# A pad of 320 bytes at one end of the on-chip memory, and one buffer fewer for a scratch tile of the query rotation

## The chip, the cores and the metric

The kernel runs on one core of one Trainium2 chip. The time is device microseconds of that core, the median of several executions. Beside it stands one profiled execution, from which all rows of the trace come.

## The reference

One step of a one-layer hybrid encoder in float32. A prompt of 1024 frames and 8 running streams of 16 frames (1152 rows, nine tiles of 128) go through the same layer:

```
h = rmsnorm(x) @ w_in                  # split in xr, gate, q, k, v, qi, ki, wi
y_a = rglru(conv(xr)) * gelu(gate)     # recurrent group, width 512
y_b = attention of rope(rmsnorm(q)), rope(rmsnorm(k)), v
      over the 256 (132) keys that qi, ki, wi select by their scores
x = x + concat(y_a, y_b) @ w_out
x = x + (silu(g) * u) @ w_ffn_out      # g, u = rmsnorm(x) @ w_ffn_in, inner width 2816
```

Keys, values, index keys and the recurrent states are outputs too.

## The kernel before

The program is one core's, recorded by a helper, so nearly all vector, scalar and pool instructions carry line 66 and nearly all matmuls line 207 (`mm`), 212 (`mm4`, plain float32) or 217 (transposes); they are told apart by the tiles they write and read.

**Matmuls.** A float32 factor is split in a high and a low part (`split`, `hi`, `lo`), both of a 4-byte type that the matmul takes as it is, and one product is three matmuls (`mm3`): high by high and both mixed ones. Each matmul loads its 128 stationary columns anew. In a row of the trace `ps<-hf,w 128*128 128x384` the moving tile comes first (`hf`, 384 columns), then the stationary one (`w`, 128 columns); in `ps<-w,a` the moving tile is `w2` (shown as `w`), the stationary one `a`.

**Stages, by the trace's time.** 0 to 73 us: norm, keys and values (`wk`). To 185: index scores (`ki`, `qeo`). To 372: the recurrent group (`h` moving, `w` stationary), with the first half of the queries beside it. To 408: the second half of the queries (`q_tile`, nine tiles of 24 matmuls with 256 moving columns, `w,h`). 408 to 475: the first half of the output product (`out_tile_a`, `wa,yF`), while the keys are rotated (`k_rope`) and the masks of the selection are made. To 653: attention. To 713: second half of the output product (`out_tile`, `w,rest`) with the second norm. To 1543: the feed-forward part (`ffn`), 22 slices of 128 inner columns. `ffn1` makes one slice: 2 weight columns, 3 thirds of the rows, 24 matmuls each, 144 in all. `ffn2` adds two slices into the result: 108 matmuls of 512 moving columns, eleven times.

**Rotation buffers.** `rope` takes a scratch tile, lets POOL write its two halves (`rp<-qn,tab`), and VectorE multiplies the query tile by the table (`qn<-qn,tab`) and adds the scratch tile (`qn<-qn,rp`):

```python
t2 = pool.tile([128, H, 64], F32, tag="rp", name="rp", bufs=bufs)
```

With two buffers POOL may write the scratch tile of the next query tile while VectorE still has to read that of this one. `k_rope` already calls it with one.

**Where tiles lie.** The memory of a partition is allotted from two ends. The lower end holds `h`, `hf`, `rest`, `smr`, `acc`, `ki`; the upper end, from the top down, the raw weights, the eight slots `w`, then what each stage needs. In `ffn` two weight tiles in ten and one `w2` tile in six go to free room in `rest` at the lower end (`slot1`, `slot2`):

```python
k = slots[0] % 10
if k % 5:
    return self.wslot(shape)
return rest[k // 5].rearrange("p (a x n) -> p a x n", a=4, x=2)
```

The built program's addresses, as remainder modulo 512 bytes (the row steps inside these tiles are whole multiples of 512 bytes, except `wk`, whose rows are 1312 bytes):

| tile | lies at | remainder |
|---|---|---|
| `h`, `hf`, `rest`, `smr`, `ki` | 1696 to 124,575 | 160 |
| `w` (8 slots), `raw` | 188,384 to 229,343 | 480 |
| `w2`, `a`, `sg` in `ffn` | 141,280 to 188,383 | 480 |
| `wk` | 109,792 to 130,783 | 224 at its start |
| `vhl` | 155,168 | 32 |
| `k1`, `k2` | 90,688 and 98,880 | 64 |

**Order.** Generators are interleaved by a planner in the kernel (`run`), and a scheduler of the framework then orders every engine's queue. Each engine takes its queue in order.

Of the kernel before, what the change touches and what calls it, by code (L numbers as in the profile page):

```python
# [9 lines left out]
F32 = mybir.dt.float32  # L10
# [71 lines left out]
class Kernel:  # L82
# [183 lines left out]
    def build(self, upto=99):  # L266
        ctx, tc, nc, I, O = self.ctx, self.tc, self.nc, self.I, self.O
        L = "left"
        R = "right"
# [2 lines left out]
        self.dram = ctx.enter_context(tc.tile_pool(name="dram", bufs=1, space=bass.MemoryType.DRAM))  # L272
        right, yst, mid, tka, kist = (ExitStack() for _ in range(5))
        pool = lambda st, name, side, bufs=1: st.enter_context(tc.tile_pool(name=name, bufs=bufs, side=side))
        self.raw = pool(right, "raw", R, 2)
        self.wr = pool(right, "wr", R, self.SLOTS)
        yF_p = pool(yst, "yF", R)
# [930 lines left out]
    def q_tile(self, i, half, tp, gq):  # L1208

        nc = self.nc  # L1210
        w, = yield from self.wait_w(("q", half))
        tab = self.tables(tp, i, gq, 2)
        pq = self.ps()
        for d in range(ND):
            ww = w[d // 2]
            self.mm3(pq[:, :256], self.h_lhs(i, d, 0), self.h_lhs(i, d, 1), ww[:, d % 2, 0, :],
                     ww[:, d % 2, 1, :], d == 0, d == ND - 1)
        if i == NT - 1:
            self.wused -= 4
        self.n_q += 1  # L1220
        self.begin()
        x = self.qn[:, i, half * 256:half * 256 + 256]
        nc.scalar.activation(x, pq[:, :256], AF.Copy)
        t = self.end()
        for h in range(4):
            sq = tp.tile([128, 64], BF16, tag="sq", name="sq")
            nc.scalar.activation(sq, pq[:, h * 64:h * 64 + 64], AF.Square, scale=0.125,
                                 accum_out=self.qss[:, i, 4 * half + h:4 * half + h + 1])
        yield 0.0
        yield from self.until(t)  # L1230
        x = x.rearrange("p (h d) -> p h d", h=4)
        self.rope(x, x, tab, 4, tp)

    def q_norm(self, tp):

# [515 lines left out]
```

## Time and profile before

| | |
|---|---|
| median of 3 runs | 1549.23 us (1546.99 to 1549.92) |
| the profiled execution's own time | 1549.64 us |
| its span, first to last instruction | 1547.9 us |
| TensorE busy | 1479.1 us (96%), 7786 matmuls |
| VectorE, ScalarE, POOL busy | 866.1, 619.5, 269.3 us |
| feed-forward stage | 712.8 to 1543.4 us |

The rows below come from views of that one execution. In the timeline of an engine each row merges consecutive instructions of one kind; the difference between the start of a row and the start of the next one, divided by the count, is the time from one matmul to the next. That is the rate; the duration of a single matmul (338 ns mean for `hf,w`) is longer, as matmuls overlap.

### The profile page before, as it was taken

The page shows a single profiled execution, that of the slowest core. Times are in us where ns is not written, and L with a number is a line of the kernel's source. Part 1 is how long each engine was busy: PE and PEld are TensorE (multiplying, and loading weights), DVE is VectorE, ACT ScalarE, POOL GpSimd, SP SyncE. Part 2 cuts the span into 40 slices and gives each one's busy share as a digit, 9 for nine tenths or more (in the row PEclk, how much of TensorE's full clock was granted, in tenths as well). Part 3 has the DMA queues.
Part 4 walks back from the last instruction along what each step waited for, and adds up shares of the span by engine and source line. Part 5 has one row for each costly group of instructions (what it writes and reads, how often), then busy time and mean ns, then how long its engine had stood idle before and what let it go on. Part 6 is the DMA issues. An engine that isn't in the chain of part 4 may idle for free.

```text
span 1547.9 us, 20878 instructions
## 1 busy us (share of the span) xinstructions
PE 1479.1 (96%) x7786; PEld 1314.3 (85%) x7786; DVE 866.1 (56%) x1904; ACT 619.5 (40%) x1481; POOL 269.3 (17%) x425
## 2 busy tenths in 40 slices
PE   6889899889997999999999999999999999999998
PEld 6877688778745788889999898989898989898987
DVE  7556899899968987677233334242424242515133
ACT  5447988978315878655202020202121111111100
POOL 4214233334764545200000000000000000000000
PEclk8999899999998999999999999999999999999999
DMA  7201111011410002123102020202011111101003
GB/s 240 58 16 31 46 37 30 4 31 57 153 41 11 1 28 58 39 56 92 46 0 82 1 82 4 79 20 63 27 55 31 51 42 41 55 28 55 28 0 122
DMA packets 95093, 75.24 MB, mean 49 GB/s; under 512 B 13380, under 2 KB 85828, under 8 KB 94992
## 3 DMA queue, kind: packets, MB, share of 16 engines
q1 hardware_dynamic: 94992, 73.91, 15.8%
q8 instruction: 61, 1.00, 0.3%
q14 instruction: 40, 0.33, 0.1%
HBM read 67.62 MB, written 6.27 MB: 48 GB/s over the span
## 4 chain that ended last, share of the span: by engine, by line
PE 75%; DVE 10%; ACT 6%; issue 4%; POOL 2%; DMA 2%; SPq 0%; ACTq 0%; DVEq 0%; POOLq 0%
PE ps L207 68%; PE ps L212 4%; DVE junk L66 4%; PE ps L217 3%; ACT jk L66 3%; DVE tk_cand L66 2%; ACT L66 1%; DVE tr L66 1%; ACT tr L66 1%; DMA gk<-in_k_norm_dram 0%; ACT relu L66 0%; DMA x<-in_x_prompt_dram 0%; POOL m L66 0%; DVE s L66 0%; DVE m L66 0%
## 5 line engine op out<-in xcount | busy, mean ns | idle before, releaser
L207 PE MATMUL ps<-hf,w 128*128 128x384 f32 x2556 | 460.5, 338 | 0.0
L207 PEld LDWEIGHTS ps<-hf,w 128*128 128x128 f32 x2556 | 451.5, 187 | 0.8
L207 PE MATMUL ps<-w,a 128*128 128x512 f32 x999 | 239.1, 390 | 0.0
L66 DVE TENSOR_TENSOR acc<-ps,acc 128x512 f32<-128x512 f32 x234 | 161.0, 690 | 120.3 <-PE ps L207 119.2
L207 PEld LDWEIGHTS ps<-w,a 128*128 128x128 f32 x999 | 187.4, 188 | 40.1
L66 ACT ACTIVATE w<-raw 128x512 fp32r<-128x512 f32 x124 | 75.2, 628 | 300.5 <-PE ps L207 220.9
L66 DVE TENSOR_TENSOR sg<-ps,sg 128x384 f32<-128x384 f32 x66 | 36.7, 557 | 279.9 <-PE ps L207 279.3
L66 DVE TENSOR_TENSOR w<-raw,w 128x512 fp32r<-128x512 f32 x116 | 76.8, 687 | 85.2 <-ACT w L66 85.0
L66 ACT ACTIVATE a<-sg 128x384 fp32r<-128x384 f32 x66 | 34.5, 523 | 220.8 <-DVE sg L66 220.8
L207 PE MATMUL ps<-hf,rest 128*128 128x384 f32 x612 | 114.5, 334 | 0.0
L66 ACT ACTIVATE jk<-s,tk_cand 128x384 bf16<-128x384 f32 (+3 forms) x128 | 99.5, 777 | 32.4 <-DVE tk_cand L66 29.6
L207 PE MATMUL ps<-h,w 128*128 128x384 f32 x576 | 107.1, 343 | 0.0
L207 PEld LDWEIGHTS ps<-hf,rest 128*128 128x128 f32 x612 | 106.9, 188 | 0.2
L207 PEld LDWEIGHTS ps<-h,w 128*128 128x128 f32 x576 | 100.8, 188 | 3.9 <-ACT relu L66 0.2
L207 PE MATMUL ps<-w,h 128*128 128x256 f32 (+1 forms) x600 | 97.0, 318 | 0.0
L207 PEld LDWEIGHTS ps<-w,h 128*128 128x128 f32 x600 | 84.3, 192 | 6.6 <-issue 0.2
L66 ACT ACTIVATE sg<-ps 128x384 f32<-128x384 f32 x66 | 32.1, 486 | 122.0 <-PE ps L207 122.0
L212 PE MATMUL ps<-wa,yF 128*128 128x512 f32 x144 | 64.9, 605 | 2.7 <-DVE tk_cnt L66 2.7
L66 POOL TENSOR_SCALAR m<-m,mx 128x128 f32<-128x128 f32 (+7 forms) x64 | 51.7, 816 | 53.6 <-DVE mx L66 42.7
L212 PEld LDWEIGHTS ps<-wa,yF 128*128 128x128 f32 x144 | 27.1, 194 | 36.0 <-issue 30.3
L207 PE MATMUL ps<-smr,vhl 128*128 128x512 f32 x162 | 54.0, 418 | 2.3 <-ACT smr L66 1.4
L66 ACT ACTIVATE m<-m,mx 128x128 f32<-128x128 f32 (+7 forms) x64 | 49.3, 770 | 16.1 <-DVE mx L66 15.7
(266 smaller groups left out, 2142.0 us busy)
## 6 DMA issues: line engine op xcount, KB each, us to landing
raw<-in_w_ffn_in_dram SPq DMA_DIRECT2D x44, 512.0 KB, 4.8
raw<-in_w_ffn_out_dram SPq DMA_DIRECT2D x22, 512.0 KB, 3.6
raw<-in_w_in_dram SPq DMA_DIRECT2D x16, 512.0 KB, 5.0
out_dram<-acc SPq DMA_DIRECT2D x9, 512.0 KB, 2.6
x<-in_x_prompt_dram SPq DMA_DIRECT2D x8, 512.0 KB
acc<-in_x_prompt_dram SPq DMA_DIRECT2D x8, 512.0 KB
tab<-in_rope_dram SPq DMA_DIRECT2D x43, 64.0 KB, 1.8
wa<-in_w_out_dram SPq DMA_DIRECT2D x4, 512.0 KB
```

What stands on the lines that cost most here:

```text
L66: return f(*args, **kw)
L207: self.nc.tensor.matmul(out, lhsT, rhs, start=start, stop=stop)
L212: self.nc.tensor.matmul(out, lhsT, rhs, start=start, stop=stop)
L217: self.nc.tensor.transpose(out, in_, self.ident[0:n, 0:n])
```

## The change

A pool with one tile of 80 floats per partition (320 bytes), which nothing uses, is opened at the upper end ahead of all others, so everything at the upper end lies 320 bytes lower. The rotation of the query tiles takes one scratch buffer (1024 bytes) where it took two, which leaves the stage of the recurrent group and the queries the room; the tiles of that stage then lie 704 bytes higher.

```diff
         pool = lambda st, name, side, bufs=1: st.enter_context(tc.tile_pool(name=name, bufs=bufs, side=side))
+        pool(right, "pad", R).tile([128, 80], F32, name="pad_r")
         self.raw = pool(right, "raw", R, 2)
...
         x = x.rearrange("p (h d) -> p h d", h=4)
-        self.rope(x, x, tab, 4, tp)
+        self.rope(x, x, tab, 4, tp, bufs=1)
```

Remainders after: `w`, `raw`, `w2`, `a`, `sg` 160 (were 480), `vhl` 224 (was 32), `k1` and `k2` 256 (were 64), `wk` 416 at its start (was 224); the lower end keeps 160. Counts of instructions stay as they were on TensorE, and up to about 375 us of the trace every queue keeps its order. From the query tiles to the first attention tile the scheduler orders some queues differently.

POOL, late in the query tiles: `rp` is the scratch tile, `tab` the table of sines and cosines, scaled by `gq`; `tt`, `tr` and `yF` are tiles of the recurrent group (minus: before, plus: after).

```order
-L66 TENSOR_TENSOR rp<-qn,tab 128x4x32 x4
+L66 TENSOR_TENSOR rp<-qn,tab 128x4x32 x2
 L66 TENSOR_SCALAR tt<-tt 128x384 x3
 L66 MEMSET tr 128x1
-L66 TENSOR_TENSOR tab<-tab,gq 128x128
+L66 TENSOR_TENSOR rp<-qn,tab 128x4x32 x2
 L66 MEMSET tt 128x8
-L66 TENSOR_TENSOR rp<-qn,tab 128x4x32 x2
-L66 TENSOR_TENSOR tab<-tab,gq 128x128
-L66 TENSOR_TENSOR rp<-qn,tab 128x4x32 x2
+L66 TENSOR_TENSOR tab<-tab,gq 128x128
 L66 TENSOR_TENSOR yF<-yF,tr 128x384
```

Before, POOL wrote the scratch tiles of two query tiles one after the other; now other work, or a wait for VectorE, stands between two of them, and every later query tile stands one to three places further back.

VectorE, where the masks of the first selection group end and the first results of the output product are added (`jk`, `tk_cnt`: the mask; `acc`: the result tile):

```order
-L66 SCALAR_TENSOR_TENSOR ps<-jk_912,ps 128x256
-L66 TENSOR_TENSOR acc<-ps,acc 128x512
+L66 SCALAR_TENSOR_TENSOR ps<-jk_916,ps 128x256
+L66 TENSOR_TENSOR qn<-qn,tab 128x256
 L66 TENSOR_TENSOR tk_cnt<-tk_cnt,ps 128x1
 L66 TENSOR_TENSOR acc<-ps,acc 128x512
-L66 TENSOR_TENSOR qn<-qn,tab 128x256
+L66 TENSOR_TENSOR qn<-qn,rp 128x256
 L66 TENSOR_SCALAR tk_cnt<-tk_cnt 128x1
-L66 TENSOR_TENSOR qn<-qn,rp 128x256
```

Before, the fifteenth of 18 query tiles had been rotated ahead of this point and the sixteenth stood behind it; now the fourteenth stands here.

TensorE, in the same stage, before and after:

```order
L212 MATMUL ps<-wa,yF 128x512 x12
L217 MATMUL ps<-ident,kn 128x128
L212 MATMUL ps<-wa,yF 128x512 x6
L217 MATMUL ps<-ident,kn 128x128
L212 MATMUL ps<-wa,yF 128x512 x6
```

```order
L212 MATMUL ps<-wa,yF 128x512 x8
L217 MATMUL ps<-ident,kn 128x128
L212 MATMUL ps<-wa,yF 128x512 x8
L217 MATMUL ps<-ident,kn 128x128
L212 MATMUL ps<-wa,yF 128x512 x8
```

The transposes of the rotated keys (`ident,kn`) stand at slightly other places among the matmuls of the output product; nothing else moves on TensorE.

## Rows read from the trace of the kernel before

**Rows 1.** The page: granted TensorE clock by slices, chain by line.

```profile
PEclk8999899999998999999999999999999999999999
...
PE ps L207 68%; PE ps L212 4%; DVE junk L66 4%; PE ps L217 3%; ACT jk L66 3%; DVE tk_cand L66 2%; ACT L66 1%; DVE tr L66 1%; ACT tr L66 1%; DMA gk<-in_k_norm_dram 0%; ACT relu L66 0%; DMA x<-in_x_prompt_dram 0%; POOL m L66 0%; DVE s L66 0%; DVE m L66 0%
```

**Rows 2.** Stretches: length, busy PE, PEld, DVE, ACT, POOL (counts), clock, DMA, GB/s.

```profile
712.80:1543.40 830.60, 830.60 (x4373) 781.36 (x4371) 295.33 (x471) 143.78 (x268) 0.00 (x0) 1.00 0.15 45
...
408.00:480.00 72.00, 66.08 (x163) 29.23 (x161) 49.90 (x109) 14.10 (x48) 40.68 (x72) 0.98 0.11 34
```

**Rows 3.** Timeline of PE, feed-forward: start us, us, what, count.

```profile
739.58 2.25 PE L207 MATMUL ps<-hf,rest 128*128 128x384 f32 x12
741.66 6.52 PE L207 MATMUL ps<-hf,w 128*128 128x384 f32 x36
748.02 2.25 PE L207 MATMUL ps<-hf,rest 128*128 128x384 f32 x12
...
790.22 24.64 PE L207 MATMUL ps<-w,a 128*128 128x512 f32 x108
814.70 4.40 PE L207 MATMUL ps<-hf,w 128*128 128x384 f32 x24
...
865.34 1.52 PE L207 MATMUL ps<-w,a 128*128 128x512 f32 x6
866.70 0.86 PE L207 MATMUL ps<-rest,a 128*128 128x512 f32 x3
867.40 2.22 PE L207 MATMUL ps<-w,a 128*128 128x512 f32 x9
869.46 0.86 PE L207 MATMUL ps<-rest,a 128*128 128x512 f32 x3
```

**Rows 4.** Matmul groups by shape: count, busy us, mean ns, idle before.

```profile
L207 PE MATMUL ps<-hf,w 128*128 128x384 f32 x2556 | 460.5, 338 | 0.0
...
L207 PE MATMUL ps<-h,w 128*128 128x384 f32 x576 | 107.1, 343 | 0.0
L207 PE MATMUL ps<-w,h 128*128 128x256 f32 x432 | 54.4, 286 | 0.0
L207 PE MATMUL ps<-rest,a 128*128 128x512 f32 x189 | 54.2, 394 | 0.0
L207 PE MATMUL ps<-smr,vhl 128*128 128x512 f32 x162 | 54.0, 418 | 2.3 <-ACT smr L66 1.4 <-DVE smr L66 0.9
L207 PE MATMUL ps<-w,rest 128*128 128x512 f32 x216 | 52.3, 396 | 0.2 <-DVE rest L66 0.2
```

**Rows 5.** Timeline of PE: keys and values, query tiles, second half of the output product.

```profile
47.98 11.11 PE L207 MATMUL ps<-wk,h 128*128 128x328 f32 x72
58.93 0.38 PE L217 MATMUL ps<-ident,kr 128*64 128x128 f32 x2
...
399.14 8.73 PE L207 MATMUL ps<-w,h 128*128 128x256 f32 x72
407.71 13.89 PE L212 MATMUL ps<-wa,yF 128*128 128x512 f32 x32
...
678.08 8.50 PE L207 MATMUL ps<-w,rest 128*128 128x512 f32 x36
686.42 1.03 PE L217 MATMUL ps<-ident,xs 128*128 128x128 f32 x8
```

**Rows 6.** Timeline of PE: the one pause in the first half of the output product.

```profile
425.25 4.41 PE L212 MATMUL ps<-wa,yF 128*128 128x512 f32 x6 [2.67 <-DVE tk_cnt L66]
```

**Rows 7.** Timelines of DVE and POOL: last query rotation, key rotations with one buffer.

```profile
439.34 0.45 DVE L66 TENSOR_TENSOR qn<-qn,rp 128x256 f32<-128x256 f32 x1
...
459.38 0.29 DVE L66 TENSOR_TENSOR kn<-kn,rp 128x128 f32<-128x128 f32 x1
...
445.04 0.60 POOL L66 TENSOR_TENSOR rp<-kn,tab 128x64 f32<-128x64 f32 x2
...
448.35 0.60 POOL L66 TENSOR_TENSOR rp<-kn,tab 128x64 f32<-128x64 f32 x2
```

## The prediction

> **What bounds the kernel now.** I read the clock and the chain first, then the busy times of single stretches, then TensorE's timeline. The chain that ended last is 68% matmuls of line 207, and TensorE's granted clock is full in nearly every slice after the start [rows 1]. In the feed-forward stage this goes to the limit: 830.60 of 830.60 us are busy on TensorE at clock 1.00, with VectorE at 295 us and ScalarE at 144 [rows 2]. So nothing but the time from one matmul to the next sets this stage, more than half of the span. A few ns for each of its 4373 matmuls is the whole matter, and I look for what makes two matmuls of one shape differ there.
>
> Starts divided by counts give it [rows 3]. Twelve `hf,rest` take 739.58 to 741.66, 173.3 ns each; the 36 `hf,w` behind them take 741.66 to 748.02, 176.7 ns. Both stream the same 384 columns of `hf`. What differs is where the stationary tile lies: `rest` has remainder 160 like `hf`, `w` has 480. Pure `w,a` (both 480) take 790.22 to 814.70 for 108, 226.7 ns. Where weights lie in `rest`, three `rest,a` (160 against 480) take 866.70 to 867.40, 233.3 ns, and nine `w,a` behind them 867.40 to 869.46, 228.9 ns. So with equal remainders 384 columns cost 173.3 ns and 512 cost 226.7 ns, at 2.4 GHz in both cases their columns plus 13.3 ns, and a piece with unequal pairs in it costs 2 to 7 ns more for each. That is one reading of the rows; another stands among the rivals.
>
> **The change part by part.** The counts on TensorE stay, so each term is a number of matmuls times a difference of rates. The sum is made against the profiled execution, 1549.64 us (span 1547.9, so 1.7 us lie outside the span, and they stay); it stands 0.4 us above the median.
>
> *First feed-forward products.* From 814.70 to 865.34 two slices run, 288 matmuls in 50.64 us, 175.8 ns on average [rows 3], single `hf,rest` among them. After the change all have remainder 160 on both sides: 288 times 173.3 ns is 49.92 us, 0.72 us less. 22 slices of 144 are 3168 such matmuls, 2556 of them `hf,w` [rows 4], eleven blocks of 288: 11 times 0.72 = **7.9 us**. TensorE waits for nobody here, so all of it lies on the path. From below: if only `hf,w` of the sampled row gained half of its excess, 2556 times 1.7 ns, 4.3 us. From above: all 2556 at the sampled excess, 2556 times 3.4 ns, 8.7 us.
>
> *Second feed-forward products.* Where `rest` takes part, twelve matmuls take 866.70 to 869.46, 2.76 us, 230.0 ns each, and 108 take 24.84 instead of 24.48 us. There are 189 `rest,a` [rows 4]; 27 make a whole round (three of every twelve), so seven of the eleven rounds are mixed. Afterwards `a`, `w2` and `rest` all have 160: 7 times 0.36 = **2.5 us**. Nearly sure if the reading is right, since the six `w,a` before the mixed ones (865.34 to 866.70, 226.7 ns) show the goal in the same round.
>
> *Second half of the output product.* 36 `w,rest` (480 against 160) take 678.08 to 686.42, 231.7 ns [rows 5]; 226.7 is the goal. 216 of them [rows 4] times 5.0 ns: **1.1 us**.
>
> *Recurrent group.* 576 `h,w` of 384 columns [rows 4] change from unequal to equal. They run in short pieces between pauses, so I take a quarter of what the feed-forward rows would give (576 times 3.4 ns = 2.0 us): **0.5 us**, with 0 and 2.0 as bounds.
>
> *Query tiles.* Here the sign turns. 72 `w,h` with 256 columns take 399.14 to 407.71, 119.0 ns [rows 5], while 256 columns and the 13.3 ns that the longer shapes show would be 120.0. 432 of them [rows 4] times 1.0 ns: **0.4 us lost**, between 0 and 1.
>
> *Attention.* `vhl` goes from 32 to 224 against 160, `k1` and `k2` move with `w`; pairs that were unequal stay unequal. I take nothing; the largest group, 162 `smr,vhl` [rows 4], at up to 7 ns (the excess of `rest,a` over `w,a`) bounds it at 1.1 us either way.
>
> *The missing rotation buffer.* With two buffers POOL writes the next scratch tile while VectorE reads this one; with one it goes in turns. What that costs shows in the key rotations, which have one already: 445.04 to 448.35, 3.3 us from one write to the next [rows 7]. Behind the waiting POOL stand the tables of the next query tiles and the steps of the recurrent group; behind VectorE's `qn<-qn,rp` stand the masks, the additions to `acc` and the keys, since each queue is taken in order. TensorE needs them late: the one pause in the first half of the output product is 2.67 us and ended by VectorE's `tk_cnt` [rows 6]. In the new order one and a half query tiles fewer stand ahead of that `tk_cnt`: two instructions of 0.45 us each [rows 7] and a bit, so the pause can shrink by up to some 1.4 us. On the other hand the last query rotation, which ended at 439.8 before [rows 7], comes about one round trip of 3.3 us later, the keys behind it with it. POOL is busy 40.7 and VectorE 49.9 of 72 us there [rows 2], so neither is full and most of the delay is absorbed. I price the stage at **1.0 us lost**, nearer to the existing pause than to a whole round trip; bounds are 1.4 gained and 4.0 lost (a round trip plus what it leaves cold in the clock, which is 0.98 there [rows 2]).
>
> *Sum.* 7.9 + 2.5 + 1.1 + 0.5 − 0.4 − 1.0 = 10.6 us gained. The profiled execution would go to 1539.0, and the median from 1549.2 to about 1538.6 us.
>
> **What the skill says against it.** The row first: stationary tiles in another place change the rate of the same moving tile by 3.4 ns [rows 3]. The Trainium skill, "TensorE: Matmul & The Clock Gate", section "Step-by-step: what each phase is for", says that TensorE has two independent read ports, so that loading the next weights takes nothing from the running matmul. By that the place of the weights would not matter, and the first rival below would hold. The traces bear against it as far as they go, since unequal tiles are slower everywhere that I sampled 384 or 512 columns. The same page gives for back-to-back matmuls 2.5 ns above the columns; by it the goal for 384 columns would be 162.5 ns and the first term an estimated 42 us. No row reaches this, also those with equal remainders, so the rows decide.
>
> **The rivals.**
>
> *It isn't the remainder.* `h`, `hf` and `rest` share not only a remainder but also the lower end of the memory, while `w`, `w2` and `a` share the upper end. `hf,rest` and `w,a` are then fast because both tiles lie at one end, and a pad of 320 bytes does nothing. Then the matmul terms vanish and the rotation's 1.0 us stays: about 1550 us. Against it speaks `wk`, which lies at the lower end like `h` and whose rows of 1312 bytes run through many remainders: 72 `wk,h` of 328 columns take 47.98 to 58.93, 152.1 ns [rows 5], where 328 columns and 13.3 ns would be 150.0. So tiles at one end are slow too when their remainders differ, by 2 ns. But early in the span other things run beside it, and 2 ns is little. Chance 0.12.
>
> *Half of it.* The excess of `hf,w` depends on how loads and matmuls fall against each other; with equal remainders 173.3 was seen in pieces of twelve, and a whole slice may settle between. With half of the first two terms, the gain is 5.4 us, 1543.8 us. Chance 0.10; it counts as faster.
>
> *Slower: the single buffer holds up the keys.* If POOL and VectorE really go in turns for the nine tiles of the second half, nine round trips of 3.3 us are 30 us, instead of running beside each other, and the key rotations, which ended at 459.7 [rows 7], would start so much later. The stretch ends at 480 [rows 2] with attention's scores needing the keys: 20 us of room at most, so 10 us or more of pause at TensorE. It decides from where the added pause exceeds the 11.6 us that the matmul terms give back; at nine full round trips plus the masks behind them 15 us come together, and the time is 1552.6. For it speaks that VectorE has 109 instructions in 72 us there [rows 2], each of which can stand between POOL's write and its read. Against it: the order on TensorE and VectorE moves by one or two tiles only, and the last rotation of a query ended 20 us ahead of that of the keys [rows 7]. Chance 0.06.
>
> **How the numbers follow.** The forecast of 1538.6 us has 0.68, half of it 0.10, the remainder without effect 0.12, the held-up keys 0.06, and 0.04 remain for gains above 14 us (recurrent group and attention at their upper bounds). 0.2% is 3.1 us, about what a measurement of this kernel can tell from no change. Faster by more than that is the forecast, its half and the large gains, 0.82; the effectless remainder is the same except for a small part, 0.12; slower 0.06. The forecast's own range follows from its bounds: 1535.0 with the recurrent group at 2.0 (1.5 more), the rotation gaining 1.4 instead of losing (2.4 more), no loss at 256 columns (0.4 more), 1534.3 together, of which hardly all come at once; 1543 with the first term at 4.3 and the rotation a little worse. For 8 times in 10 the range reaches past the half to 1546, which leaves out the effectless remainder, the slower case and the largest gains.
>
> **What would show it.** Right: `hf,w` pieces of 36 at 173.3 ns like those from `rest`, a feed-forward stage of about 820 us, still fully busy; rounds with `rest,a` at 24.48 us for 108; `w,rest` at 226.7 ns; TensorE's pause in the first half of the output product within 4 us of before, and key rotations ending before 465. Wrong: `hf,w` still at 176.7 ns and `rest,a` at 233 though their remainders are now equal, which would leave the memory's end as the cause; `w,h` of 256 columns well above 120 ns, which would make equality a loss for short shapes; or long pauses of TensorE behind `kn` or `qn`, with POOL waiting for VectorE at `rp`.

## The result, and the profile after

The changed kernel takes 1537.52 us, the median of six runs (1535.5 to 1540.66), against 1547.15 us of the kernel before (six runs too, among them the three that gave 1549.23). The ratio is 0.9936, with a 95% interval from 0.9922 to 0.9950; that is 9.6 us less, and 7.7 to 12.1 us by the interval. 1538.6 us had been forecast, in a range from 1535.0 to 1546.0.

First the feed-forward stage and the first half of the output product, as stretches of the changed kernel (length, busy PE, PEld, DVE, ACT, POOL with counts, clock, DMA, GB/s); then the chain by line from its page:

```profile
708.10:1529.20 821.10, 821.06 (x4373) 773.88 (x4371) 295.42 (x472) 143.82 (x268) 0.00 (x0) 1.00 0.15 46
404.70:472.40 67.70, 63.35 (x156) 27.80 (x155) 47.96 (x105) 10.23 (x42) 41.88 (x72) 1.00 0.13 37
```

```profile
PE ps L207 66%; DVE junk L66 4%; PE ps L217 3%; ACT jk L66 3%; PE ps L212 3%; DVE tk_cand L66 2%; DVE tr L66 1%; ACT L66 1%; DMA x<-in_x_prompt_dram 1%; ACT tr L66 1%; POOL rp L66 1%; DVE ti L66 1%; DVE qn L66 1%; DMA gk<-in_k_norm_dram 0%; ACT relu L66 0%
```

The feed-forward stage has as many matmuls as before and TensorE is busy in all of it, but it takes 821.10 us where it took 830.60 [rows 2]: **9.5 us less, at the same clock of 1.00**. The output product's first half takes 67.7 us; from the first `wa,yF` at 407.71 [rows 5] to 475.3 us it took 67.6 before. New in the list are POOL's `rp` and VectorE's `ti` and `qn`, with 1% each [rows 1].

The profiled execution itself took 1535.5 us, the fastest of the six. Its span is 14.3 us shorter than that of before. Of the 4.8 us beyond the feed-forward stage 4.7 lie ahead of it, and a second profile of the same kernel (below) starts that stage at 711.1 us, not at 708.1. So 3.0 of them are the spread of single executions. The length of the stage, in contrast, was the same to 0.1 us in all profiles of one placement of tiles.

TensorE's timeline in the changed kernel (start us, us, what, count; the time from one matmul to the next is again the difference of starts by the count):

```profile
809.29 4.35 PE L207 MATMUL ps<-hf,w 128*128 128x384 f32 x24
813.48 2.24 PE L207 MATMUL ps<-hf,rest 128*128 128x384 f32 x12
815.56 6.40 PE L207 MATMUL ps<-hf,w 128*128 128x384 f32 x36
821.80 2.24 PE L207 MATMUL ps<-hf,rest 128*128 128x384 f32 x12
...
859.24 1.55 PE L207 MATMUL ps<-w,a 128*128 128x512 f32 x6
860.63 0.85 PE L207 MATMUL ps<-rest,a 128*128 128x512 f32 x3
861.32 2.20 PE L207 MATMUL ps<-w,a 128*128 128x512 f32 x9
863.36 0.84 PE L207 MATMUL ps<-rest,a 128*128 128x512 f32 x3
864.04 2.20 PE L207 MATMUL ps<-w,a 128*128 128x512 f32 x9
866.08 0.84 PE L207 MATMUL ps<-rest,a 128*128 128x512 f32 x3
```

The 36 `hf,w` now take 815.56 to 821.80, 173.3 ns each, like the twelve `hf,rest` ahead of them (2.08 us, 173.3 ns); they were 176.7 [rows 3]. The block of 288 takes 809.29 to 859.24, 49.95 us where it took 50.64. Three `rest,a` and nine `w,a` take 863.36 to 866.08, 2.72 us or 226.7 ns each, where they took 2.76.

The query tiles and the second half of the output product:

```profile
396.00 8.88 PE L207 MATMUL ps<-w,h 128*128 128x256 f32 x72
404.71 13.90 PE L212 MATMUL ps<-wa,yF 128*128 128x512 f32 x32
...
673.56 8.43 PE L207 MATMUL ps<-w,rest 128*128 128x512 f32 x36
681.82 1.03 PE L217 MATMUL ps<-ident,xs 128*128 128x128 f32 x8
```

72 `w,h` of 256 columns take 8.71 us, 121.0 ns each: 2.0 ns more than before [rows 5]. 36 `w,rest` take 8.26 us, 229.4 ns: 2.3 ns less. Each of these pieces begins with one long interval behind other work, by the starts of the single matmuls 208 and 200 ns (`w,h`, before and after) and 315 and 314 ns (`w,rest`). Without it `w,h` goes from 117.7 to 120.0 ns and `w,rest` from 229.3 to 227.1.

The rotation, in the timelines of TensorE, VectorE and POOL of the changed kernel (in brackets the pause ahead and what ended it):

```profile
422.46 2.84 PE L212 MATMUL ps<-wa,yF 128*128 128x512 f32 x6 [2.88 <-DVE acc L66]
...
444.28 3.67 PE L212 MATMUL ps<-wa,yF 128*128 128x512 f32 x8 [1.48 <-DVE k L66]
```

```profile
440.00 0.42 DVE L66 TENSOR_TENSOR qn<-qn,rp 128x256 f32<-128x256 f32 x1
...
456.72 0.29 DVE L66 TENSOR_TENSOR kn<-kn,rp 128x128 f32<-128x128 f32 x1
```

```profile
416.74 1.24 POOL L66 TENSOR_TENSOR rp<-qn,tab 128x128 f32<-128x128 f32 x2 [0.42 <-DVE qn L66]
```

Counted from the first `wa,yF`, the last query rotation ends at 440.42 − 404.71 = 35.7 us; before, it was 439.79 − 407.71 = 32.1 [rows 5, 7]. It comes **3.6 us later**, about one round trip. The last key rotation ends at 52.3 us of that count, where it ended at 52.0. POOL waits for VectorE's `qn` at two `rp`, 1.5 us together. On TensorE the one pause is 2.88 us where it was 2.67 [rows 6], and a second one of 1.48 us has come in, ended by VectorE's `k`; yet the stage is only 0.1 us longer than before.

### The profile page after: what moved, and what is told of

Its sections match the earlier page's. It is cut to its first block, busy times and chain, and to the rows that moved or that the text cites. A ratio compares the mean times of both kernels' runs of the same rounds, so it can differ in the third digit from the quotient of the medians.

```text
span 1533.6 us, 20876 instructions
## 1 busy us (share of the span) xinstructions
PE 1466.4 (96%) x7786; PEld 1305.5 (85%) x7786; DVE 867.4 (57%) x1904; ACT 619.2 (40%) x1481; POOL 270.2 (18%) x425
## 4 chain that ended last, share of the span: by engine, by line
PE 72%; DVE 12%; ACT 7%; issue 4%; POOL 2%; DMA 2%; SPq 0%; ACTq 0%; DVEq 0%; POOLq 0%
PE ps L207 66%; DVE junk L66 4%; PE ps L217 3%; ACT jk L66 3%; PE ps L212 3%; DVE tk_cand L66 2%; DVE tr L66 1%; ACT L66 1%; DMA x<-in_x_prompt_dram 1%; ACT tr L66 1%; POOL rp L66 1%; DVE ti L66 1%; DVE qn L66 1%; DMA gk<-in_k_norm_dram 0%; ACT relu L66 0%
## 5 line engine op out<-in xcount | busy, mean ns | idle before, releaser
L207 PE MATMUL ps<-hf,w 128*128 128x384 f32 x2556 | 453.1, 334 | 0.0
L207 PEld LDWEIGHTS ps<-hf,w 128*128 128x128 f32 x2556 | 444.2, 188 | 0.7
L66 ACT ACTIVATE jk<-s,tk_cand 128x384 bf16<-128x384 f32 (+3 forms) x128 | 99.4, 777 | 32.1 <-DVE tk_cand L66 29.5
L66 ACT ACTIVATE sg<-ps 128x384 f32<-128x384 f32 x66 | 32.1, 486 | 119.0 <-PE ps L207 119.0
```

What stands on the lines that cost most here:

```text
L66: return f(*args, **kw)
L207: self.nc.tensor.matmul(out, lhsT, rhs, start=start, stop=stop)
```

## The experiments

All kernels from here on have the changed kernel's order on every queue or, where it is said, that of the kernel before; within each of the two sets only the place of tiles differs. "Stage" is the feed-forward stage, from its first `hf,w` to its last `w,a`. Each median is compared with runs of the kernel before on the same chip, whose medians are 1546.8 to 1547.5 us.

### Order and buffer alone

```diff
-        pool(right, "pad", R).tile([128, 80], F32, name="pad_r")
```

> One scratch buffer, no pad: every queue has the order of the changed kernel, every address at the upper end of the memory that of the kernel before. Theory (the equal remainders gave the gain, the rotation costs next to nothing): hf,w at 176 ns, rest,a at 233 ns, feed-forward stage 830 to 831 us, first half of the output product 67.5 to 68 us as in both profiles, whole time 1547 to 1548.5 us. Rival (the new order or the freed buffer gave it): the stage and the whole as with the change, about 821 and 1538 us.

Measured: 1548.07 us, ratio 1.0005 (0.9995 to 1.0014). The stage and the output product's first half, and the group `hf,w` (count, busy us, mean ns of one, idle before):

```profile
711.10:1541.70 830.60, 830.55 (x4373) 781.34 (x4371) 295.38 (x472) 143.82 (x268) 0.00 (x0) 1.00 0.15 45
406.20:473.20 67.00, 64.79 (x155) 28.36 (x154) 47.30 (x102) 10.22 (x42) 41.27 (x71) 0.97 0.12 36
```

```profile
L207 PE MATMUL ps<-hf,w 128*128 128x384 f32 x2556 | 460.5, 338 | 0.0
```

The stage is back at 830.60 us and the group at 460.5 us, as before [rows 4]. So the gain comes from addresses alone, and neither the order nor the single buffer has a part in it. What these two cost can't be told from nothing by this run. The output product's first half is 0.5 us shorter than had been expected.

### The pad at the other end

```diff
-        pool(right, "pad", R).tile([128, 80], F32, name="pad_r")
...
+        pool(ctx, "pad", L).tile([128, 80], F32, name="pad_l")
         self.hblk = ctx.enter_context(tc.tile_pool(name="h", bufs=6, side=L))
```

> The pad of 320 bytes at the lower end instead, one scratch buffer: h, hf, rest and smr go from 160 to 480, the upper end stays at 480. Theory (only the difference of the remainders counts): hf,w 173.4, rest,a 227 ns, feed-forward stage 821 us, 1536 to 1540 us, as with the pad at the upper end. Rival (the tiles of the upper end had to move, or the remainder has to be 160): hf,w 176 ns, stage 830 us, 1546 to 1549 us.

Measured: 1537.77 us, ratio 0.9944 (0.9928 to 0.9961). The stage:

```profile
709.20:1530.30 821.10, 821.09 (x4373) 773.87 (x4371) 295.34 (x471) 143.83 (x268) 0.00 (x0) 1.00 0.15 46
```

Now the upper end lies where it lay before, the lower end has moved by 320 bytes, and the stage is 821.10 us again. It is the distance of the two ends that counts, not the place of either, and not that tiles share one end of the memory.

### The pad in parts of the kernel before

In the first, only the second and the third third of `hf` move; in the second, only `w2`, `a` and `sg`. Both keep two scratch buffers and the order of the kernel before.

```diff
+        pool(ctx, "pad", L).tile([128, 80], F32, name="pad_l")
         hf_p = ctx.enter_context(tc.tile_pool(name="hf", bufs=4, side=L))
```

> The kernel before with two scratch buffers and its order; a pad of 320 bytes at the lower end is allotted only ahead of the second and third third of hf, so these two have 480 like w, while the first third and rest keep 160. Theory: in one slice, hf,w of the second and third thirds at 173.4 ns, of the first third still at 176.4, and hf,rest of the second and third thirds up from 173.4 to 175 or 176. 1704 matmuls gain 3.0 ns and 408 lose 2 to 3: feed-forward stage about 826.5 us, the whole 1542 to 1544.5 us. Rivals: if the end of the memory counts, nothing changes (830.6 us, 1547); if tiles of the moving side alone count, hf,rest gains or stays as well.

Measured: 1543.41 us, ratio 0.9979 (0.9969 to 0.9988). The stage and the two groups of the first products:

```profile
709.50:1536.10 826.60, 826.57 (x4373) 776.97 (x4371) 295.40 (x471) 143.77 (x268) 0.00 (x0) 1.00 0.15 45
```

```profile
L207 PE MATMUL ps<-hf,w 128*128 128x384 f32 x2556 | 456.1, 336 | 0.0
...
L207 PE MATMUL ps<-hf,rest 128*128 128x384 f32 x612 | 114.6, 336 | 0.0
```

826.6 us came as forecast, but not by the forecast's own terms. The mean difference of successive starts is 174.0 ns for `hf,w` with equal remainders and 175.9 with unequal ones. But the `hf,rest` with 480 against 160, which should have become slower, take 173.3 ns, no more than with equal remainders. The group's busy time, 114.6 us, is within 0.1 us of that of the kernel before:

```profile
L207 PE MATMUL ps<-hf,rest 128*128 128x384 f32 x612 | 114.5, 334 | 0.0
```

**With 384 columns unequal remainders can be as fast as equal ones**: 480 against 160 is, 160 against 480 isn't.

```diff
+        pool(right, "pad", R).tile([128, 80], F32, name="pad_r")
         with tc.tile_pool(name="ffn", bufs=2, side=R) as tp:
             self.ffn(tp)
```

> The kernel before with its order and two scratch buffers; a pad of 320 bytes at the upper end is allotted only ahead of the feed-forward stage's own pool, so w2, a and sg have 160 like rest, while w keeps 480. Theory: rest,a from 233.3 to 227 ns, the rounds with rest back to 24.5 us for 108, hf,w unchanged at 176 ns, feed-forward stage 2.5 us shorter (828.1), the whole about 1544.7 us. Rival (the place of the tiles doesn't matter for rest,a, or a loss at a's other uses): 830.6 us, 1547 us.

Measured: 1545.01 us, ratio 0.9989 (0.9979 to 0.9999). The stage, and a part of TensorE's timeline in a round with `rest`:

```profile
709.90:1538.10 828.20, 828.19 (x4373) 781.05 (x4371) 295.46 (x471) 143.82 (x268) 0.00 (x0) 1.00 0.15 45
```

```profile
866.55 0.84 PE L207 MATMUL ps<-rest,a 128*128 128x512 f32 x3
867.23 2.20 PE L207 MATMUL ps<-w,a 128*128 128x512 f32 x9
869.27 0.84 PE L207 MATMUL ps<-rest,a 128*128 128x512 f32 x3
```

The stage is 2.4 us shorter, and twelve matmuls take 866.55 to 869.27, 2.72 us. By the starts of all matmuls 2.0 of the 2.4 us lie in the second feed-forward products; 0.4 lie in the first ones, though their own tiles have not moved. In the changed kernel the 9.5 us divide into 2.0 for the second products and 7.5 for the first ones.

### Other sizes of the pad

One scratch buffer in all, and only the size of the pad at the upper end differs:

```diff
-        pool(right, "pad", R).tile([128, 80], F32, name="pad_r")
+        pool(right, "pad", R).tile([128, 16], F32, name="pad_r")
```

(16 floats are 64 bytes; then 72, 64, 32, 48 and 24 floats.)

> Pad of 64 bytes instead of 320, one scratch buffer: w has remainder 416, h, hf and rest 160, so they differ by 256 bytes. Theory (512 bytes is the period): hf,w stays at 175 to 178 ns, feed-forward stage 828 to 831 us, 1546 to 1549 us. Rival (any pad moves the upper end into a better place, or the period is 256 or 128 bytes): hf,w 173.4 ns, stage 821 us, about 1538 us.

> Pad of 288 bytes, one scratch buffer: w has remainder 192, h, hf and rest 160, 32 bytes apart. Version A (the remainders must be equal): hf,w 175 to 178 ns, stage 828 to 831 us, 1546 to 1549 us. Version B (near is enough): hf,w about 173.5 to 174 ns, stage 821 to 823 us, 1537 to 1540 us. I hold A for likelier, 65 to 35.

The next four were written after the pads of 64 and 288 bytes had been measured.

> Pad of 256 bytes, one scratch buffer: w has remainder 224 modulo 512 where it has 480 without a pad; modulo 256 it is 224 both times. After the pad of 64 bytes did what that of 320 does, the theory is that 256 bytes are the period and a pad of 256 is as good as none: hf,w 176.4, rest,a 233.3 ns, feed-forward stage 830.6 us, 1547 to 1549 us. Rival (512 bytes are the period, and the pad of 64 met a second good place by chance): hf,w somewhere between 173 and 178 ns with no reason to be 176.4, and a stage other than 830.6 by 2 us or more.

> Pad of 128 bytes: w has 352, so modulo 256 the moving tile hf stands 64 bytes ahead of the stationary w, and not 64 behind as before. Theory (the sign of the difference counts, as the products of the second and third third of hf with rest showed in the run with the pad ahead of hf: 480 against 160, 173.3 ns): hf,w 173.3, rest,a 230 ns (as w,rest before, which has the same difference), w,rest 233 ns (as rest,a before); feed-forward stage 821.5 to 823 us, 1538 to 1541 us. Rival (only equality helps): hf,w 176 ns, stage 828 to 831 us, 1546 to 1549 us.

> Pad of 192 bytes: w has 288, 128 bytes from h, hf and rest. If 128 bytes were the period, all is as with the change: hf,w 173.4, rest,a 227 ns, stage 821 us, 1537 to 1540 us. If it is 256, half a period apart: rest,a and w,rest above 229 ns and a stage of 823 to 831 us, 1540 to 1549 us. I hold the second for likelier, 70 to 30, since 64 bytes behind and 64 ahead gave different rates.

> Pad of 96 bytes: w has 384, so modulo 256 hf is 32 bytes ahead of w (with the pad of 288 it was 32 behind: hf,w 173.4, hf,rest 175.3, rest,a 233.6, w,rest 233.7 ns). Theory (matmuls of 512 columns pay for 32 bytes either way, those of 384 columns hardly): rest,a and w,rest 233 to 234 ns, hf,w 173 to 175, stage 823 to 826 us, 1540 to 1544 us. Rival (384 columns pay on this side): hf,w 176 to 178 ns, stage 830 to 834 us, 1547 to 1551 us.

The stretches of 64 and of 256 bytes, with their groups `hf,w`:

```profile
709.60:1530.70 821.10, 821.09 (x4373) 773.89 (x4371) 295.59 (x471) 143.82 (x268) 0.00 (x0) 1.00 0.15 46
```

```profile
L207 PE MATMUL ps<-hf,w 128*128 128x384 f32 x2556 | 453.1, 334 | 0.0
```

```profile
709.70:1540.30 830.60, 830.57 (x4373) 781.36 (x4371) 295.50 (x471) 143.81 (x268) 0.00 (x0) 1.00 0.15 45
```

```profile
L207 PE MATMUL ps<-hf,w 128*128 128x384 f32 x2556 | 460.5, 338 | 0.0
```

The stretches of 288, 128, 192 and 96 bytes:

```profile
712.80:1536.20 823.40, 823.40 (x4373) 775.01 (x4371) 295.26 (x471) 143.81 (x268) 0.00 (x0) 1.00 0.15 45
711.70:1536.60 824.90, 824.90 (x4373) 774.88 (x4371) 295.21 (x471) 143.93 (x268) 0.00 (x0) 1.00 0.15 45
710.80:1541.30 830.50, 830.50 (x4373) 781.20 (x4371) 295.19 (x471) 143.91 (x268) 0.00 (x0) 1.00 0.15 45
711.10:1542.20 831.10, 831.10 (x4373) 781.66 (x4371) 295.70 (x471) 143.90 (x268) 0.00 (x0) 1.00 0.15 45
```

A pad of 64 bytes does all that one of 320 does, and one of 256 does as little as none, both to 0.1 us of the stage. **The period is 256 bytes, not 512.** The remainders needn't be equal modulo 512, as they were made; `w` at 416 and `hf` at 160 are as good.

All sizes, ordered by the stage. "Ahead" is the address of `hf` minus that of `w`, modulo 256; negative, `hf` lies behind. The same holds for `rest` against `a`; `w,rest` and `w,h` have the opposite sign. The ns are means of the differences between successive starts, over all pairs of the shape without a pause or a long first interval:

| pad, bytes | ahead | stage us | `hf,w` | `hf,rest` (equal) | `w,a` (equal) | `rest,a` | `w,h` 256 columns | median us |
|---|---|---|---|---|---|---|---|---|
| 320 | 0 | 821.1 | 173.4 | 173.4 | 227.1 | 226.9 | 119.8 | 1537.52 |
| 64 | 0 | 821.1 | 173.4 | 173.4 | 227.1 | 226.9 | 119.8 | 1538.79 |
| 288 | −32 | 823.4 | 173.4 | 175.3 | 227.0 | 233.6 | 117.3 | 1542.56 |
| 128 | +64 | 824.9 | 173.3 | 175.3 | 229.4 | 229.8 | 114.6 | 1544.25 |
| 192 | 128 | 830.5 | 175.9 | 175.0 | 228.3 | 232.0 | 118.8 | 1548.35 |
| none, one buffer | −64 | 830.6 | 176.4 | 173.5 | 227.8 | 233.3 | 117.8 | 1548.07 |
| 256 | −64 | 830.6 | 176.4 | 173.5 | 227.8 | 233.3 | 117.8 | 1548.35 |
| 96 | +32 | 831.1 | 176.5 | 173.4 | 228.1 | 234.2 | 118.3 | 1548.63 |

Half a period (192 bytes) was on the slower side, so 128 bytes are no period. For 288 bytes neither version had the whole: `hf,w` is as fast as with equal remainders, while the unequal `rest,a` of 512 columns pay some 7 ns. For 96 bytes the theory failed and the rival came: `hf,w` pays on this side, 176.5 ns. For 128 bytes `hf,w` came as forecast, 173.3 ns, and `rest,a` nearly so, but the stage is 2 us above the forecast, since the means of *equal* pairs rose beside unequal ones: `hf,rest` from 173.5 to 175.3 ns, `w,a` from 227.8 to 229.4. TensorE's timeline of that kernel:

```profile
740.48 6.41 PE L207 MATMUL ps<-hf,w 128*128 128x384 f32 x36
746.72 2.27 PE L207 MATMUL ps<-hf,rest 128*128 128x384 f32 x12
748.82 6.41 PE L207 MATMUL ps<-hf,w 128*128 128x384 f32 x36
```

The unequal 36 take 6.24 us, 173.3 ns each; the equal twelve take 2.10 us, 175.0, the other way round than before [rows 3]. The starts of the single matmuls say where this is lost: in 49 of the 51 such pieces of twelve the first three stand 185, 175 or 176 and 181 or 182 ns apart, and the others, as ever, 173.3. The equal `w,a` are slow only in the rounds with `rest,a`: 231.5 ns there, 226.8 in the other rounds. So an equal pair keeps its rate, and in this kernel some 22 ns are lost at each change from an unequal piece of `hf,w` to an equal one. Why there, none of these runs tells.

Nor does the distance alone fix the rate of an unequal pair. One piece of 36 `w,rest` lies behind a short pause in the kernel before and, with the same remainders, in the kernel with one buffer and no pad:

```profile
667.93 8.64 PE L207 MATMUL ps<-w,rest 128*128 128x512 f32 x36 [0.16 <-DVE rest L66]
676.41 1.91 PE L217 MATMUL ps<-ident,xs 128*128 128x128 f32 x16
```

```profile
666.34 8.48 PE L207 MATMUL ps<-w,rest 128*128 128x512 f32 x36 [0.16 <-DVE rest L66]
674.65 1.91 PE L217 MATMUL ps<-ident,xs 128*128 128x128 f32 x16
```

It takes 8.48 us in the first and 8.31 in the second; inside the piece the matmuls stand 233.3 and 228.9 ns apart. What the matmuls of 256 columns show is that equality is not even the best place: 114.6 ns against 119.8.

### The attention's pairs too, beside the changed kernel

```diff
         self.tail = vk_p.tile([128, 4, 36], F32, name="tail")
+        vk_p.tile([128, 16], F32, name="pad_vk")
...
         self.ksT = k_p.tile([128, 2, 128], F32R, name="ksT")
+        k_p.tile([128, 8], F32, name="pad_k")
...
-        with tc.tile_pool(name="t1b", bufs=2, side=R) as tp:
+        with tc.tile_pool(name="pad_q", bufs=1, side=R) as qp, tc.tile_pool(name="t1b", bufs=2, side=R) as tp:
+            qp.tile([128, 80], F32, name="pad_q")
```

> The changed kernel again, beside the next ones on the same chip: 1535 to 1541 us, feed-forward stage 821 us.

> The changed kernel with three more pads: 64 bytes behind vhl's pool, 32 behind the keys k1 and k2, 320 ahead of the index queries' pool. Now vhl, k1, k2 and the index queries qeo have 160 too, like smr, rest, ki and the other qeo. Theory (equal remainders are worth it for every pair): smr,vhl and rest,vhl of 512 columns from about 234.5 to 227 or 228 ns, 216 of them, 1.5 us; k,qeo and ki,qeo of 384 and 512 columns 3 to 7 ns less each, about 1 us together; TensorE has pauses in these stages, so 1 to 2.5 us less than the changed kernel. Rival (these pairs are limited by something else, or the gain goes into TensorE's pauses): the same time as the changed kernel, within 1 us.

Measured: the changed kernel again 1538.85 us, ratio 0.9943 (0.9930 to 0.9955); with the three pads 1536.30 us, ratio 0.9929 (0.9914 to 0.9943). The five runs with the pads took 1535.29 to 1538.26 us, the five without 1537.43 to 1540.42, and the six of the first comparison 1535.5 to 1540.66. The first row is the group `smr,vhl` of the changed kernel's first profile, the second that of the kernel with the pads:

```profile
L207 PE MATMUL ps<-smr,vhl 128*128 128x512 f32 x162 | 53.5, 415 | 1.9 <-ACT smr L66 1.3 <-DVE smr L66 0.5
```

```profile
L207 PE MATMUL ps<-smr,vhl 128*128 128x512 f32 x162 | 53.3, 414 | 1.8 <-ACT smr L66 1.3 <-DVE smr L66 0.5
```

0.2 us in 162 matmuls, where 1.1 had been expected; from start to start (intervals under 300 ns) they went from 234.8 to 233.2 ns, not to 227. `k,qeo` of 384 columns took 12.4 us with the pads, and 12.4 and 11.8 in the two profiles of the changed kernel. So equal remainders are not worth as much for every pair. These matmuls come in short pieces between other work; what sets their rate is not shown. The attention itself took 176.7 us with the pads, and 176.9 and 178.4 in the two profiles of the changed kernel, so the 2.6 us between the medians aren't shown to come from the pads. That this version beats the changed kernel is not shown.

## Why the prediction was right, and where it wasn't

*What bounds the kernel.* Right: the stage stayed fully busy on TensorE and all that a matmul lost in time came out at the end.

*First products, 7.9 us.* Measured 7.5; the block of 288 lost 0.69 instead of 0.72 us [rows 3], and over all pairs the goal was 173.4 ns, not 173.3. Pieces of 36 keep 173.3 as pieces of twelve did, so the rival with half of the gain is out.

*Second products, 2.5 us.* Measured 2.0: a round with `rest` went from 24.83 to 24.52 us, not to 24.48, and the four rounds without it from 24.48 to 24.52.

*Second half of the output product, 1.1 us.* Mis-sized: 2.3 ns instead of 5.0, times 216 gives 0.5 us. The goal of 226.7 ns was right, the start of 231.7 was not: the sampled piece, at 678.08 in [rows 5], begins with one interval of 315 ns behind a transpose, and the other 35 average 229.3 ns before and 227.1 after.

*Query tiles, 0.4 us lost.* The sign was right, the size half: 2.0 ns times 432 are 0.9 us. The goal of 120.0, extrapolated from longer shapes, is met; the start was 117.7, not 119.0, since this piece, at 399.14 in [rows 5], begins with a long interval too, of 208 ns.

*Recurrent group, 0.5 us.* From 174.4 to 173.65 ns by the differences of starts, times 576 is 0.4 us.

*Rotation, 1.0 us lost.* The delay of one round trip was right for the last query rotation, 3.6 us for 3.3. But the keys did not come later with it, by 0.3 us only, so the rival in which the keys are held up is out; and the pause that was to shrink by up to 1.4 us is 2.88 us in one profile and 1.94 in the other, where it was 2.67. What the single buffer costs is below what single profiles tell: this stage takes 65.2 to 67.8 us in the eleven profiles with one buffer and 66.9 to 67.6 in the three with two. The medians of the two placements whose stage is again 830.6 us, one scratch buffer in both, are 1548.07 and 1548.35 us, with ratios of 1.0005 (0.9995 to 1.0014) and 1.0011 (1.0002 to 1.0021): a cost between nothing and 3 us. 1.0 fits, but it is not shown by itself, and where it lies is open.

*Sum.* 7.5 + 2.0 + 0.5 + 0.4 − 0.9 − 1.0 = 8.5 us, where the last term is the forecast's; forecast 10.6; measured 9.6 (7.7 to 12.1) and, in the second comparison, 8.8 (7.0 to 10.8) as 0.57% of 1547. The 1.1 us between 8.5 and 9.6 are less than the interval is wide, and nothing here says where they lie. The forecast time of 1538.6 started from 1549.2, and six runs of the kernel before gave 1547.15; so the time came out 1.1 us below the forecast although the gain is 1.0 us smaller.

*The reading itself.* Right where it was used and wrong as a rule. The prediction said that, with 384 and 512 columns, equal remainders modulo 512 are fast and unequal ones slow. The rows it used held one or two differences per shape, so they couldn't tell 512 from 256, nor equality from a few other good places. `wk,h`, by which I argued against the rival of the memory's ends, was a weak argument: its piece of 72, at 47.98 in [rows 5], begins with an interval of 235 ns, and the other 71 average 150.9 ns, 0.9 and not 2 above the 150.0. The rival fell all the same: with the ends kept and only the distance changed, the stage went from 821.1 to 831.1 us. Where the weights lie relative to the moving tile changed the rate by up to 7 ns a matmul. This speaks against what the Trainium skill says of two independent read ports, that loading the next weights takes nothing from the running matmul ("TensorE: Matmul & The Clock Gate", section "Step-by-step: what each phase is for"); whether it is the load that holds the matmul up, no run shows by itself.

## What to carry to other kernels

Where TensorE is busy all the time, compare the time from start to start of matmuls of one shape whose tiles lie in different places: here some 2.2 ns in each of the stage's 4373 matmuls were 9.5 us, and 64 bytes of pad would have done. Take the rate from inside a piece: one long first interval of 200 to 315 ns shifted three of the forecast's rates by 1.2 to 2.4 ns. Try several distances modulo 256 bytes on the chip and judge by the length of the busy stage, which repeats to 0.1 us, not by the whole time, which spreads by some 5 us. What is best differs by the number of columns, so weigh each shape by its count. A mixture of good and bad pairs can have a cost of its own at each change between them.

## What the runs showed of the hardware that was not expected

- The rate depends on the distance of moving and stationary tile modulo 256 bytes: pads of 64 and 320 bytes give the same stage (821.1 us), none and 256 as well (830.6).
- The sign counts: for 384 columns a moving tile 32 bytes behind or 64 ahead of the stationary one is as fast as one at no distance (173.3 to 173.4 ns); 32 ahead and 64 behind are not (176.4 to 176.5). `rest,a` of 512 columns was fast only at no distance (226.9 ns, against 229.8 or more at the others).
- With 256 columns an unequal distance is the fastest seen: 114.6 ns with the moving tile 64 bytes behind, against 119.8 at no distance.
- Behind an unequal piece, at some distances, the first three intervals of an equal one are longer (`hf,rest` 185, 176 and 182 ns with the pad of 128 bytes, then 173.3). Why is open.
- Unequal pairs with the same remainders ran at two rates behind a pause: 233.3 and 228.9 ns (`w,rest`). Why is open.
